# An encoder step with a dense pass over all experts: gelu values gated and split in their PSUM banks, a regrouped grid of gates, one one-hot factor made by ScalarE

## The chip, the cores and the metric

One core of one Trainium2 chip runs the whole program. The metric is the device time of one execution in microseconds, the lower the better; where several runs are given, it is their median. TensorE (PE) does matmuls and transposes, VectorE (DVE) elementwise work with two inputs, ScalarE (ACT) functions of one input, GpSimd (POOL) elementwise work and the issue of gathers, SyncE (SP) most of the transfers. Sums of products come out of PE in PSUM banks, everything else lives in SBUF.

## What is computed

The reference is one layer of a streaming encoder over 1024 prompt frames and 32 sample frames of 1024 channels: a token mixer (differential attention and a gated recurrence behind one projection), then PEER, a mixture of 16384 single-neuron experts with 8 heads of 16 chosen experts a frame. The change touches the second half:

```python
def blk(xs):
    q = (xs @ w_q).reshape(P_TBLOCK, P_HEADS, 2, P_DQ).astype(jnp.float32)
    s = jnp.einsum('thcd,hckd->thck', q, sub_keys.astype(jnp.float32))
    sv, si = lax.top_k(s, P_TOPK)
    comb = (sv[:, :, 0, :, None] + sv[:, :, 1, None, :]).reshape(P_TBLOCK, P_HEADS, P_TOPK * P_TOPK)
    cv, ci = lax.top_k(comb, P_TOPK)
    e = ...
    gate = jax.nn.softmax(cv, axis=-1)
    hid = jax.nn.gelu(jnp.einsum('thkd,td->thk', down[e], xs).astype(jnp.float32), approximate=False)
    return jnp.einsum('thk,thkd->td', (gate * hid).astype(xs.dtype), up[e])
```

So each frame adds, over its 128 chosen experts, gate times gelu of (expert's row of `down` dot the frame) times the expert's row of `up`.

## The kernel before, in words

The frames are nine tiles: 0 to 7 of 128 prompt frames each and "S" with the 32 sample frames. Tiles 0 to 4 (`DENSE`, 640 frames, `NV`) go through *all* experts by dense products; tiles 5, 6, S and 7 (`ROWS`) gather the rows of their chosen experts, 128 gathered rows a prompt tile and 32 for S (four frames' places side by side on the partitions), 416 in all.

**Streams.** Five generators are woven by the times that they yield: `gemm` (projection, output stages, and at its end the dense pass), `attn`, `routing` (top 16 of each head), `scatter` and `rows`. The order in which the instructions of an engine stand comes from this weave and from a scheduler over it; each engine then runs its own queue in order.

**Scatter.** For each dense tile the gates are laid on the grid of all experts. For four frames at a time (a step; 160 steps in all) one one-hot factor `ohA` (row of the expert) is made by DVE (L1126) in every second step and by ACT in the others (four times Abs, L1134, then Relu, L1135); the other factor `ohB` is made by DVE (L1126) and multiplied by the gates on POOL (L1139). PE multiplies them (L1090), ACT copies the bank to `stg` (L1091), and 16 frames at a time go to DRAM, `W_d`, laid out as [block of 8 columns, 128, frame, column].

**The dense pass** (`stage_v`) has 128 columns of 128 experts, in 32 groups of four (`JU`). For a column, `hidden` makes two halves of 320 frames: 24 matmuls into a bank (L261 to L263: a product of numbers in two parts each, high by high, low by high, high by low), and ACT puts gelu of the bank into `vg` in SBUF (L1174). `gated` multiplies `vg` by the gates `gw` on DVE, half by half (L1214; `gw` holds a frame's eight columns side by side, so one column is read at every eighth number), ACT copies the result to `vwh` (L254, 640 wide), DVE subtracts that for the low part `vwl` (L255, 640 wide). Then `down`'s weights of the group meet four columns at once: 8 pieces of the channels by 2 halves of frames are 16 products of 12 matmuls into banks `gv`, and DVE adds each to `acc` in SBUF (L1279). So a group is 384 matmuls of 320 columns, and its loop `for dq in range(4)` makes one column of the *next* group's hidden values and then four products of this group. `vwh` and `vwl` have six places (`WR`), `gv` has five banks, a sixth (`wsp`) serves the scatter and the tile S, two belong to the rows.

**Rows.** POOL issues a gather of 128 rows (L1044; four places `row`, `RB`), DVE makes the dot product with the frame (L1047), ACT gelu and gate (L1049, L1050), DVE adds the weighted row (L1031), always one row later than the dot. Columns 2 to 5 of the first hidden values lie in the place that `acc` takes later (`early`).

Of the kernel before, what the change touches and what calls it, by code (L numbers as in the profile page):

```python
# [7 lines left out]
F32 = mybir.dt.float32  # L8
# [4 lines left out]
OP = mybir.AluOpType  # L13
# [14 lines left out]
# tiles of frames that share a pass over w_in; tiles that share one over the other weights  # L28
AG = [[0, 1, 2, 3, 4], [5, 6, 7, "S"]]
CDG = [[0, 1, 2], [3, 4], [5, 6, 7, "S"]]  # L30
# tiles whose expert products run over all experts; the other ones gather the rows of theirs
# [3 lines left out]
# tiles whose scores wait in DRAM, and how many heads are routed at a time if not all  # L35
DEFER = [6, 7]
HG = {5: 2, 6: 4}
# places of weights in the rings, as they come and in two parts: output stages, then projections
RINGS = [(4, 4), (2, 3), (3, 4), (4, 4)]
SCS = [2, 2, 4, 3]  # L40
# places of the recurrence's tiles, by group
DEEP = [(2, 10), (1, 5)]
# frames on their way into the projections, by group
PRE = [2, 1]
# places of: gathered rows; expert weights, as they come and split; best halves; one-hots
RB, VR, VB, BB, OHB = 4, 3, 2, 4, 4
# engines that make the one-hot rows, in turn
AMS = "DA"
# of the splits of weights in the output stages, one in so many goes to the vector engine
CSH = 2  # L50
# banks of the large products: so many of so many in turn from the extra pool of that size
GX = (3, 6, 3)
# columns of experts whose hidden values wait in the place of the sums
GB, GE = 2, 6
# the time that a gathered row and a one-hot half step are taken to cost
GC, SC = 1.65, 1.0
# which streams keep behind the large products in which phase, and by how much less
# [10 lines left out]
def step_kernel(ctx, tc, x_prompt, x_sample, cache_kT, cache_v, state, norm1, w_in, lam_params,  # L68
# [27 lines left out]
    gb_bank, gv_bank = bank_of("gb"), bank_of("gv")  # L96
    TURN = [0]

    def gm_bank():
        """ the banks of the large products; more of them while the attention asks for none """  # L100
        TURN[0] += 1
        key = "gx" if "gx" in P and TURN[0] % GX[1] < GX[0] else "gm"
        return P[key].tile([128, 512], F32, name="gm", tag="gm")
# [7 lines left out]
    # ---------------------------------------------------------------- constants  # L111
# [7 lines left out]
    runs4 = consts.tile([128, 32], F32, name="runs4")  # L119
    V.tensor_add(runs4, ident[:, 0:32], ident[:, 32:64])  # L120
    V.tensor_add(runs4, runs4, ident[:, 64:96])
    V.tensor_add(runs4, runs4, ident[:, 96:128])
# [16 lines left out]
    def masks(ct):  # L139
        """ what the attention and the recurrence need of constants """  # L140
# [1312 lines left out]
```

## Time and profile before

| what | us |
|---|---|
| median of three runs | 3577.84 (3566.3 to 3578.75) |
| span of the profiled execution, its own time | 3583.5 |
| PE busy | 3257.4 (91%) |
| DVE busy | 3063.6 (85%) |
| POOL busy | 2074.9 (58%) |
| ACT busy | 1454.3 (41%) |

The span runs from the first to the last event of the profiled execution. For that execution no other time is given, so the span stands for it; it lies 5.7 us (0.16%) above the median. The mixer takes the first 1286 us, with scatter and rows beginning beside it; the dense pass takes from about 1585 us to the end. PE is busiest over the whole, but a share over the whole says little here: the stages have different limits, so they are read one by one below.

### The profile page before, as it was taken

The page shows a single profiled execution, that of the slowest core. Times are in us where ns is not written, and L with a number is a line of the kernel's source. Part 1 is how long each engine was busy: PE and PEld are TensorE (multiplying, and loading weights), DVE is VectorE, ACT ScalarE, POOL GpSimd, SP SyncE. Part 2 cuts the span into 40 slices and gives each one's busy share as a digit, 9 for nine tenths or more (in the row PEclk, how much of TensorE's full clock was granted, in tenths as well). Part 3 has the DMA queues.
Part 4 walks back from the last instruction along what each step waited for, and adds up shares of the span by engine and source line. Part 5 has one row for each costly group of instructions (what it writes and reads, how often), then busy time and mean ns, then how long its engine had stood idle before and what let it go on. Part 6 is the DMA issues. An engine that isn't in the chain of part 4 may idle for free.

```text
span 3583.5 us, 59911 instructions
## 1 busy us (share of the span) xinstructions
PE 3257.4 (91%) x21639; PEld 3128.0 (87%) x21639; DVE 3063.6 (85%) x6101; ACT 1454.3 (41%) x3508; POOL 2074.9 (58%) x1339
## 2 busy tenths in 40 slices
PE   7999899989998887868989988899999999999995
PEld 7989899867877886767889888899999999999994
DVE  3354468999787999999999999988989989989998
ACT  3544334445665544543333323333333333333332
POOL 2322125546444556666666577777767666776674
PEclk9999999999998998978999999999999999999997
DMA  4554364454465644478788777799888998998987
GB/s 164 166 158 149 107 215 158 152 151 152 148 217 183 206 130 150 152 249 298 258 289 296 275 271 290 266 341 351 316 315 335 337 343 296 346 338 333 336 325 265
DMA packets 357304, 880.58 MB, mean 246 GB/s; under 512 B 30960, under 2 KB 190192, under 8 KB 299664
## 3 DMA queue, kind: packets, MB, share of 16 engines
q1 hardware_dynamic: 297104, 440.52, 36.8%
q0 software_dynamic: 59904, 436.23, 33.0%
q8 instruction: 171, 2.80, 0.3%
q14 instruction: 125, 1.02, 0.1%
HBM read 784.47 MB, written 92.14 MB: 245 GB/s over the span
## 4 chain that ended last, share of the span: by engine, by line
PE 28%; DVE 19%; issue 2%; DMA 2%; POOL 2%; ACT 0%; POOLq 0%; ACTq 0%; DVEq 0%
PE gv L263 9%; PE gv L262 9%; PE gv L261 9%; DVE row L1047 5%; DVE xp L1031 5%; DVE vg L1214 2%; DVE acc L1279 2%; DMA ur<-in_p_up_dram 2%; DVE vwl L255 2%; POOL row L1044 1%; DVE oh L967 1%; POOL dl L255 1%; DVE ef L972 1%; POOL ul L255 0%; DVE si L902 0%
## 5 line engine op out<-in xcount | busy, mean ns | idle before, releaser
L1044 POOL DMA_INDIRECT row<-in_p_rows_dram,ei x384 | 559.8, 1458 | 340.2 <-DVE xp L1031 172.2
L255 POOL TENSOR_TENSOR wl<-wr,wh 128x1024 fp32r<-128x1024 f32 x160 | 397.3, 2494 | 532.2 <-ACT wh L254 483.0
L261 PE MATMUL gv<-vxh,dh 128*128 128x320 f32 x2048 | 646.5, 316 | 42.4 <-DVE acc L1279 23.6
L263 PE MATMUL gv<-vxh,dl 128*128 128x320 f32 x2048 | 644.8, 316 | 34.8 <-POOL dl L255 34.7
L261 PE MATMUL gv<-vwh,uh 128*128 128x320 f32 x2048 | 636.2, 311 | 14.1 <-ACT uh L254 8.3
L262 PE MATMUL gv<-vwl,uh 128*128 128x320 f32 x2048 | 636.8, 311 | 12.4 <-DVE vwl L255 12.3
L262 PE MATMUL gv<-vxl,dh 128*128 128x320 f32 x2048 | 642.3, 314 | 0.0
L263 PE MATMUL gv<-vwh,ul 128*128 128x320 f32 x2048 | 633.9, 310 | 1.1 <-POOL ul L255 1.0
L1047 DVE CUSTOM_DVE_ANT_0 row<-row,xg 128x1024 f32<-128x1024 f32 x416 | 627.0, 1507 | 3.1 <-DMA sc<-scs 2.3
L1031 DVE SCALAR_TENSOR_TENSOR xp<-row,hid,xp 128x1024 f32<-128x1024 f32 x412 | 527.8, 1281 | 78.2 <-ACT hid L1050 78.0
L1049 ACT ACTIVATE hid<-hid 128x1 f32<-128x1 f32 x416 | 84.0, 202 | 936.1 <-DVE hid L1047 926.3
L255 POOL TENSOR_TENSOR ul<-ur,uh 128x512 fp32r<-128x512 f32 x256 | 359.7, 1407 | 135.2 <-ACT uh L254 125.6
L261 PEld LDWEIGHTS gv<-vxh,dh 128*128 128x128 f32 x2048 | 393.5, 192 | 50.1 <-DVE acc L1279 27.3
L263 PEld LDWEIGHTS gv<-vxh,dl 128*128 128x128 f32 x2048 | 392.7, 192 | 43.1 <-POOL dl L255 42.0
L255 POOL TENSOR_TENSOR dl<-dr,dh 128x512 fp32r<-128x512 f32 x256 | 365.1, 1433 | 82.0 <-ACT dh L254 73.9
L261 PEld LDWEIGHTS gv<-vwh,uh 128*128 128x128 f32 x2048 | 386.7, 189 | 17.1 <-ACT uh L254 9.3
L262 PEld LDWEIGHTS gv<-vwl,uh 128*128 128x128 f32 x2048 | 386.9, 189 | 16.5 <-DVE vwl L255 16.5
L262 PEld LDWEIGHTS gv<-vxl,dh 128*128 128x128 f32 x2048 | 393.9, 192 | 0.0
L263 PEld LDWEIGHTS gv<-vwh,ul 128*128 128x128 f32 x2048 | 386.3, 189 | 2.7 <-POOL ul L255 2.5
L1139 POOL TENSOR_TENSOR ohB<-ohB,tr 128x512 f32<-128x512 f32 x160 | 195.0, 1224 | 264.3 <-DVE ohB L1126 201.5
L1214 DVE TENSOR_TENSOR vg<-vg,gw 128x320 f32<-128x320 f32 x248 | 253.4, 1022 | 27.7 <-ACT vg L1174 17.5
L261 PE MATMUL gm<-xh,wh 128*128 128x320 f32 (+1 forms) x768 | 254.0, 331 | 0.0
(328 smaller groups left out, 7490.5 us busy)
## 6 DMA issues: line engine op xcount, KB each, us to landing
dr<-in_p_downT_dram SPq DMA_DIRECT2D x256, 256.0 KB
ur<-in_p_up_dram SPq DMA_DIRECT2D x256, 256.0 KB
wr<-in_w_in_dram SPq DMA_DIRECT2D x88, 512.0 KB
W_d<-stg SPq DMA_DIRECT2D x40, 1024.0 KB
gw<-W_d SPq DMA_DIRECT2D x32, 1280.0 KB
wr<-in_p_wq_dram SPq DMA_DIRECT2D x48, 512.0 KB
wr<-in_w_out_dram SPq DMA_DIRECT2D x24, 512.0 KB
wr<-in_w_a_dram SPq DMA_DIRECT2D x12, 512.0 KB
```

The lines of the kernel that those rows point to most:

```text
L255: (lo_engine or G).tensor_tensor(out=l, in0=src, in1=h.bitcast(F32), op=OP.subtract)
L261: PE.matmul(out, lh, rh, start=(i == 0), stop=False)
L262: PE.matmul(out, lh, rl, start=False, stop=False)
L263: PE.matmul(out, ll, rh, start=False, stop=(i == n - 1))
L967: V.tensor_tensor(out=oh[:T], in0=cf[:T, h].unsqueeze(2).to_broadcast([T, 16, NCAND]), in1=iota_c[:T].unsqueeze(1).to_broadcast([T, 16, NC ...
L1031: V.scalar_tensor_tensor(out=acc, in0=row[:, D:], scalar=hid[:, k:k + 1], in1=acc if k else first, op0=OP.mult, op1=OP.add)
L1044: G.indirect_dma_start(out=row, out_offset=None, in_=p_rows, in_offset=bass.IndirectOffsetOnAxis(ap=ei[:, k:k + 1], axis=0))
L1047: V.tensor_tensor_reduce(out=row[:, 0:D], in0=row[:, 0:D], in1=xt, scale=1.0, scalar=0.0, op0=OP.mult, op1=OP.add, accum_out=h)
L1049: A.activation(h, h, AF.Gelu)
L1139: G.tensor_tensor(out=bm, in0=bm, op=OP.mult, in1=tr[:, 2, xs].unsqueeze(2).to_broadcast([128, 4, 128]))
L1214: V.tensor_mul(gh, gh, G_[h][:, :, j])
L1279: V.tensor_add(acc[:, db, cs], acc[:, db, cs], ps[:, :CHUNK])
```

## The change

- **Values in banks.** From column 6 on, gelu writes back into its PSUM bank; the gate is multiplied on the bank (bank in, bank out); high and low parts are split from it in two pieces of 320 instead of one of 640. There is no `vg` any more, and a bank is free only when both parts have been read. Every sixth bank of the dense pass is now `wsp`'s, so there are six. Columns 0 to 5 use `early`.
- **Gates by runs of 16.** `W_d` and `gw` are laid out as [.., run, column, 16 frames]; a column is read in runs of 16 numbers, and `stg` is written accordingly.
- **One-hot factor.** `ohA` is made by ACT in all 160 steps: 80 DVE instructions go, and 320 Abs and 80 Relu come to ACT.
- **Rows.** Five places for gathered rows, and the add follows two rows behind the dot. For S, three transfers and three adds take the place of a product with a constant. The routing of the `ROWS` tiles starts only after that of all dense tiles is done with.

```diff
-RB, VR, VB, BB, OHB = 4, 3, 2, 4, 4
+RB, VR, VB, BB, OHB = 5, 3, 2, 4, 4
...
+    def gv_bank():
+        TURN[0] += 1
+        pool, tag = (wsp, "ws") if PHASE[0] and TURN[0] % 6 == 0 else (P["gv"], "gv")
+        return pool.tile([128, 512], F32, name="gv", tag=tag)
...
-                if late:
-                    add(*late)
-                late = (k, row)
+                if len(late) > 1:
+                    add(*late.pop(0))
...
-                for c in range(2):
-                    ps = ws_bank()
-                    PE.matmul(ps[:T], runs4, full[:, c * 512:(c + 1) * 512], start=True, stop=True)
-                    V.tensor_add(ht[:T, c * 512:(c + 1) * 512], ht[:T, c * 512:(c + 1) * 512], ps[:T])
+                pw = wide("runs")
+                V.tensor_add(ht[:T], ht[:T], acc[:T])
+                for g, part in enumerate((pw[:, 0:D], pw[:, D:], sq)):
+                    SP.dma_start(out=part[:T], in_=full[(g + 1) * T:(g + 2) * T])
+                    V.tensor_add(ht[:T], ht[:T], part[:T])
...
-    W_d = dram([128 // JB, 128, NV, JB], "W_d")
+    W_d = dram([128 // JB, 128, NV // SB, JB, SB], "W_d")
...
+                   or (t in ROWS and not all(x in DONE for x in DENSE))
...
-                    if AMS[(s0 + q) // 4 % len(AMS)] == "A":
-                        for u in range(4):
-                            c = s0 + q + u
-                            A.activation(am[:, u], iota_r, AF.Abs, bias=tr[:, 3, c:c + 1])
-                        A.activation(am, am, AF.Relu, bias=1.0, scale=-1.0)
-                    else:
-                        equal(am, 0)
-                    equal(bm, 1)
+                    for u in range(4):
+                        c = s0 + q + u
+                        A.activation(am[:, u], iota_r, AF.Abs, bias=tr[:, 3, c:c + 1])
+                    A.activation(am, am, AF.Relu, bias=1.0, scale=-1.0)
...
-        if GB <= e < GE:
-            g = VX["early"][:, e - GB]
-        else:
-            g = wk.tile([128, NV], F32, name="vg", tag="vg", bufs=GB)
+        VX[e] = []
         for cs in CS:
             ps = gv_bank()
...
-            A.activation(g[:, cs], ps[:, :CHUNK], AF.Gelu)
-        VX[e] = g
+            g = VX["early"][:, e, cs] if e < GE else ps[:, :CHUNK]
+            A.activation(g, ps[:, :CHUNK], AF.Gelu)
+            VX[e].append(g)
...
-                g = VX[e]
-                for h in range(2):
-                    gh = g[:, h * (n // 2):(h + 1) * (n // 2)]
-                    V.tensor_mul(gh, gh, G_[h][:, :, j])
...
-                split(wh, wl, g, V)
+                for cs, g, gates in zip(CS, VX[e], G_.values()):
+                    gt = g.rearrange("p (m s) -> p m s", s=SB)
+                    V.tensor_tensor(out=gt, in0=gt, in1=gates[:, :, j], op=OP.mult)
+                    split(wh[:, cs], wl[:, cs], g, V)
```

How the program's order moves is shown at the end of one group of the dense pass. First DVE's queue before, over the last four products of one group (`acc` sums, `gv` banks, `row` and `xp` the gathered rows, `vwl` low parts of the next group's hidden values; the numbers tell one buffer from another):

```order
L1279 TENSOR_TENSOR acc_17249<-acc_17249,gv_33348 128x320
L1031 SCALAR_TENSOR_TENSOR xp_29497<-row_30330,hid_29496,xp_29497 128x1024
L1279 TENSOR_TENSOR acc_17249<-acc_17249,gv_33362 128x320
L1047 ISA row_30336,hid_29496<-row_30336,xg_29494 128x1024
L1047 ISA hid_29496 128x1
L1279 TENSOR_TENSOR acc_17249<-acc_17249,gv_33382 128x320
L255 TENSOR_TENSOR vwl_33176<-vg_33120,vwh_33175 128x640
L1279 TENSOR_TENSOR acc_17249<-acc_17249,gv_33396 128x320
L255 TENSOR_TENSOR vwl_33339<-vg_33283,vwh_33338 128x640
L1031 SCALAR_TENSOR_TENSOR xp_29497<-row_30336,hid_29496,xp_29497 128x1024
```

The low parts of two columns of the next group are taken from `vg` in SBUF, in two pieces. The changed kernel's queue at the end of a group:

```order
L1274 TENSOR_TENSOR acc_17575<-acc_17575,gv_32455 128x320
L1274 TENSOR_TENSOR acc_17575<-acc_17575,gv_32503 128x320
L1047 ISA row_31377,hid_29894<-row_31377,xg_29892 128x1024
L1047 ISA hid_29894 128x1
L1274 TENSOR_TENSOR acc_17575<-acc_17575,gv_32469 128x320
L1031 SCALAR_TENSOR_TENSOR xp_29895<-row_31377,hid_29894,xp_29895 128x1024
L255 TENSOR_TENSOR vwl_32283<-gv_32230,vwh_32282 128x320
L255 TENSOR_TENSOR vwl_32283<-gv_32256,vwh_32282 128x320
L255 TENSOR_TENSOR vwl_32442<-gv_32389,vwh_32441 128x320
L1274 TENSOR_TENSOR acc_17575<-acc_17575,gv_32489 128x320
L255 TENSOR_TENSOR vwl_32442<-gv_32415,vwh_32441 128x320
```

They are now taken from banks (`gv_32230`, `gv_32256`, `gv_32389`, `gv_32415`) in four pieces, all behind the sum of the next to last product (`gv_32469`), so four banks are held until here.

PE's queue before, at the turn from the next to last product of a group (`gv_33382`) to the last one (`gv_33396`), with the semaphores that each row waits for:

```order
L261 MATMUL gv_33382<-vwh_32683,uh_33378 128x320
L262 MATMUL gv_33382<-vwl_32684,uh_33378 128x320
L263 MATMUL gv_33382<-vwh_32683,ul_33379 128x320
L261 MATMUL gv_33396<-vwh_32194,uh_33378 128x320 [waits Activation_49]
L262 MATMUL gv_33396<-vwl_32195,uh_33378 128x320
L263 MATMUL gv_33396<-vwh_32194,ul_33379 128x320
```

The last product's bank waits only for ACT, which had emptied it as a hidden half long before. The same turn after the change, from `gv_32469` to `gv_32489`:

```order
L261 MATMUL gv_32469<-vwh_31786,uh_32451 128x320
L262 MATMUL gv_32469<-vwl_31787,uh_32451 128x320
L263 MATMUL gv_32469<-vwh_31786,ul_32452 128x320
L261 MATMUL gv_32489<-vwh_31295,uh_32485 128x320 [waits DVE_49]
L262 MATMUL gv_32489<-vwl_31296,uh_32485 128x320
L263 MATMUL gv_32489<-vwh_31295,ul_32486 128x320
```

Its first matmul now waits for DVE; what it waits for is the sum of the bank of the product directly ahead, since no other bank is free. And the turn behind the last product, where the next group's hidden half begins:

```order
L261 MATMUL gv_32489<-vwh_31786,uh_32485 128x320
L262 MATMUL gv_32489<-vwl_31787,uh_32485 128x320
L263 MATMUL gv_32489<-vwh_31786,ul_32486 128x320
L261 MATMUL gv_32553<-vxh_16916,dh_32543 128x320 [waits DVE_49]
L262 MATMUL gv_32553<-vxl_16917,dh_32543 128x320
L263 MATMUL gv_32553<-vxh_16916,dl_32544 128x320 [waits Pool_49]
```

That first matmul also waits for DVE, for the low part `vwl_32283` of the earlier column. In the changed program this pattern stands in each of the 31 groups that make hidden values for a next one.

Counted in the two programs: ahead of the first sum of the dense pass stand 31 dots of gathered rows before and 46 after; from there to the end of the eighth group 97 and 111. The last gathered row stands at the program's end before, and in group 28 (of 0 to 31) after.

## Rows read from the trace of the kernel before

**Rows 1.** Windows by stage: stretch, length, busy (count) of PE PEld DVE ACT POOL, PEclk, DMA share, GB/s.
```profile
744.00:1300.00 556.00, 494.42 (x3343) 438.94 (x3341) 488.88 (x1156) 306.33 (x736) 283.06 (x167) 0.94 0.56 173
1300.00:1706.00 406.00, 319.18 (x1967) 303.09 (x1966) 382.36 (x954) 193.63 (x458) 257.79 (x161) 0.88 0.60 204
1706.00:2243.00 537.00, 479.50 (x3076) 466.06 (x3075) 536.08 (x1003) 169.12 (x435) 360.97 (x244) 0.97 0.78 280
2243.00:2370.00 127.00, 116.65 (x772) 114.53 (x771) 120.91 (x158) 41.69 (x106) 100.83 (x65) 0.97 0.81 295
2370.00:3397.00 1027.00, 1018.73 (x6917) 1013.79 (x6916) 932.92 (x1205) 368.46 (x956) 719.66 (x512) 1.00 0.90 330
3397.00:3584.00 187.00, 142.84 (x955) 139.85 (x953) 164.62 (x235) 58.60 (x162) 115.55 (x82) 0.89 0.80 299
```

**Rows 2.** Windows, an undisturbed stretch of three and a half groups, columns as in rows 1.
```profile
2400.00:2600.00 200.00, 200.00 (x1366) 200.00 (x1365) 181.60 (x237) 74.89 (x193) 147.33 (x105) 1.00 0.91 334
```

**Rows 3.** Groups of DVE by form in 1706 to 2243: busy, mean ns, idle before.
```profile
L1047 DVE CUSTOM_DVE_ANT_0 row<-row,xg 128x1024 f32<-128x1024 f32 x99 | 155.4, 1570 | 0.0
...
L1214 DVE TENSOR_TENSOR vg<-vg,gw 128x320 f32<-128x320 f32 x64 | 73.1, 1144 | 0.0
...
L255 DVE TENSOR_TENSOR vwl<-vg,vwh 128x640 fp32r<-128x640 f32 x33 | 49.0, 1486 | 0.4 <-ACT vwh L254 0.4
```

**Rows 4.** Waits of PE in 1706 to 2243: us in total, times, longest.
```profile
PE gv L261 <- DVE acc L1279: 28.0, 17, 5.3
```

**Rows 5.** Timeline at 3545, the last matmul of the last product.
```profile
3545.54 0.31 PE L263 MATMUL gv<-vwh,ul 128*128 128x320 f32 x1
```

**Rows 6.** Groups of DVE by form in 3546 to 3584.
```profile
L1047 DVE CUSTOM_DVE_ANT_0 row<-row,xg 128x1024 f32<-128x1024 f32 x7 | 13.8, 1965 | 0.4 <-DMA row<-in_p_rows_dram,ei 0.4
L1031 DVE SCALAR_TENSOR_TENSOR xp<-row,hid,xp 128x1024 f32<-128x1024 f32 x7 | 9.0, 1280 | 0.0
```

**Rows 7.** Groups of DVE by form in 744 to 1300.
```profile
L1126 DVE TENSOR_TENSOR ohA<-iota_r,tr 128x512 f32<-128x512 f32 x48 | 38.2, 796 | 6.7 <-PE ws L1090 6.5
```

**Rows 8.** Groups of ACT by form in 744 to 1300.
```profile
L254 ACT ACTIVATE wh<-wr 128x1024 fp32r<-128x1024 f32 x66 | 69.3, 1056 | 37.7 <-DMA wr<-in_p_wq_dram 13.1 <-PE gm L262 8.3 <-DMA wr<-in_w_out_dram 6.2
L1134 ACT ACTIVATE ohA<-iota_r,tr 128x128 f32<-128x128 f32 x188 | 59.7, 394 | 0.0
...
L1135 ACT ACTIVATE ohA<-ohA 128x512 f32<-128x512 f32 x47 | 29.4, 625 | 0.2
```

**Rows 9.** Groups of DVE by form in 1300 to 1706.
```profile
L1047 DVE CUSTOM_DVE_ANT_0 row<-row,xg 128x1024 f32<-128x1024 f32 x29 | 49.8, 1716 | 2.3 <-DMA sc<-scs 2.3
L1031 DVE SCALAR_TENSOR_TENSOR xp<-row,hid,xp 128x1024 f32<-128x1024 f32 x27 | 34.5, 1278 | 10.4 <-ACT hid L1050 10.4
L1126 DVE TENSOR_TENSOR ohA<-iota_r,tr 128x512 f32<-128x512 f32 x32 | 32.1, 1004 | 1.4 <-PE ws L1090 1.4
```

**Rows 10.** One line's and one tile's instructions, whole program: min/median/max ns.
```profile
L1279 DVE TENSOR_TENSOR acc<-acc,gv x496: 423/476/514, 1716.4 to 3549.5; 128x320 f32<-128x320 f32 x166
...
L1214 DVE TENSOR_TENSOR vg<-vg,gw x248: 702/805/2767, 1586.0 to 3496.6; 128x320 f32<-128x320 f32 x124
```

**Rows 11.** Timeline at 3149, end of one product: start, us, instruction, idle before.
```profile
3148.83 0.31 PE L263 MATMUL gv<-vwh,ul 128*128 128x320 f32 x1
...
3149.18 0.49 DVE L1279 TENSOR_TENSOR acc<-acc,gv 128x320 f32<-128x320 f32 x1 [0.18 <-PE gv L263]
```

**Rows 12.** Timeline at 1801, a bank that PE waits for.
```profile
1801.44 0.47 DVE L1279 TENSOR_TENSOR acc<-acc,gv 128x320 f32<-128x320 f32 x1
...
1801.96 0.42 PE L261 MATMUL gv<-vxh,dh 128*128 128x320 f32 x1 [1.35 <-DVE acc L1279]
```

**Rows 13.** Timeline at 2161, the longest of such waits.
```profile
2161.34 0.64 PE L261 MATMUL gv<-vxh,dh 128*128 128x320 f32 x1 [5.34 <-DVE acc L1279]
```

**Rows 14.** Windows right behind these two waits, columns as in rows 1.
```profile
1801.90:1806.00 4.10, 4.04 (x27) 4.04 (x28) 4.10 (x10) 0.20 (x1) 3.62 (x3) 1.00 0.99 388
2161.30:2163.30 2.00, 1.96 (x7) 1.96 (x8) 2.00 (x17) 0.47 (x2) 1.71 (x2) 0.50 0.55 86
```

## What I expect, and why

> **What bounds the kernel now.** I read first the windows by stage [rows 1], since shares over the whole mix stages with different limits. The reader is to look in each row for the engine that fills its stretch. From 744 to 1300 us PE (494 of 556) and DVE (489) are close to each other. From 1300 to 1706 DVE is the fullest (382 of 406). From 1706 to 2243 DVE has 536 of 537 us: DVE is the limit. From 2370 to 3397 it is PE, 1019 of 1027. How many groups of the dense pass a stretch has follows from its matmuls, 384 each: 3076 are 8 groups, 772 are 2, 6917 are 18.
>
> What a group costs where only PE counts is read from a stretch without any idle time of PE: 1366 matmuls in 200 us, 146.4 ns each [rows 2], so 384 take 56.2 us. The eight groups in which DVE is the limit take 67.1 us each, the next two 63.5, the eighteen 57.1. Their excess over 56.2 is 87, 15 and 15 us: that is what relief of DVE can bring there.
>
> Next come DVE's groups by form in the stretch that it limits [rows 3]: a gathered row's dot takes 1.57 us, a gate (64 of them) 1.144, a low part of 640 columns (33) 1.486. The waits of PE there name DVE's sum into `acc` [rows 4]: a bank is not yet emptied. At the end, the last product's matmul ends at 3545.85 [rows 5], 37.7 us before the span ends, and seven gathered rows, 13.8 + 9.0 us of DVE, lie in that tail [rows 6].
>
> The sum is made against the profiled execution's 3583.5 us, 5.7 above the median of the runs; I subtract 5.7 at the end.
>
> **The change, stretch by stretch.**
>
> *744 to 1300.* Of the steps of the scatter, 48 lose their `ohA` on DVE, 0.796 us each [rows 7]: −38. ACT makes them by four Abs and a Relu, 4 × 0.394 + 0.625 = 2.2 us [rows 8]: +106, from 306 to 412 of 556, still 74%. PE's own 494 us is next in line, so DVE's 38 us can't all come off: bounds are 0 and −38, and since PE and DVE were nearly equal I take −10.
>
> *1300 to 1706.* DVE loses 32 `ohA` (−32) and most of the 10.4 us in which an add waits for its row's hidden value from ACT [rows 9], because the add now comes two rows behind (−8); a few gates get cheaper (−3). But it gets 15 more rows ahead of the first sum (46 against 31, by the program's order): 15 × (1.716 + 1.278) = +45 [rows 9]. That gives +2, and for ACT, which makes 70 us more here (194 to 264 of 406) in a queue that gelu and the splits share, I add 3: +5, between −15 and +20.
>
> *1706 to 2243, eight groups, limited by DVE.* The trace of before shows no multiplication on a bank. The nearest row is the sum into `acc`: one input from a bank, one from SBUF, 320 columns, 423/476/514 ns (shortest, middle, longest) over all 496 [rows 10]. The gate of before, both inputs in SBUF and one of them at every eighth number, has 702/805/2767. A gate on the bank has the sum's shape except that it writes to the bank, and it reads runs of 16; so I take 0.476, with the old middle value 0.805 as the upper bound. A low part of 320 columns also has one input from a bank and one from SBUF: 0.476, bounded by half of today's, 0.743. Gates: 64 × (1.144 − 0.476) = −42.8. Low parts: 33 × 1.486 = 49.0 go, 66 × 0.476 = 31.4 come, −17.6. Rows move into these groups (111 against 97 dots by the order): 14 × 1.57 + 15 × 1.28 = +41. With +7 for the wait described next, as far as it isn't hidden by DVE's own queue, this is −12; bounds: −30 (no wait, part of the rows hidden) and +27 (upper bounds of both prices).
>
> On the prices the Trainium skill bears, in "SBUF — State Buffer", section "Who interferes with whom": an instruction of VectorE with at most one input in SBUF doesn't contend with GpSimd, one with two inputs there does. The trace agrees: the sums never took over 514 ns, the gates up to 2767 [rows 10]. By the rule 0.476 holds with POOL busy as well; without it the sum would be 39 us higher, worked out below as a rival.
>
> *The wait that comes.* The order of the changed program shows it: `vwh` and `vwl` have six places and the group under way uses four, so two of the next group's columns are split at once and the other two, four banks of six, wait until the group's last product has used its places. So its last four products share two banks. The last one starts in the bank of the product directly ahead, and PE waits for DVE's sum of that. Before, those banks had been emptied a long time earlier. The price: a matmul ends 0.31 us after its start, while the next could start after 0.146, so 0.164 us are lost; DVE's sum starts 0.04 later (3148.83 + 0.31 = 3149.14, then 3149.18) and takes 0.49 [rows 11]; PE starts 0.05 after it (1801.44 + 0.47 = 1801.91, then 1801.96) [rows 12]. Together 0.74 us, if DVE is free. A dot in front of the sum can add up to 1.57; I take 0.9 on average, between 0.74 and 2.3. The next group's first hidden half waits for low parts on DVE at the same turn; the queue has these ready just as the last product ends, so I put this at nothing, with 0.3 as the other bound.
>
> *2243 to 2370, two groups.* DVE's 121 us become about 106 (a group has 8 gates and 4 low parts: 8 × 0.668 + 4 × 1.486 − 8 × 0.476 = 7.5 us less), so PE is the limit: 2 × (56.2 + 0.9) = 114 against 127, −13.
>
> *2370 to 3397, eighteen groups, limited by PE.* Relief of DVE brings nearly nothing here, the wait costs 18 × 0.9 = +16; of the 15 us lost today I let 4 go: +12, between 0 and +40.
>
> *3397 to the end.* The rows end in group 28, so their 22.8 us leave the tail; but the last sums, transposes and norms stand there too, and partly beside them: −16, and −2 for waits in the last groups. −18, between −10 and −22.
>
> S's three transfers with adds instead of a product, and the other order of routing, cost nothing: the tile's end lies beside the dense pass, and what the routing moves is in the rows counted above. The transfers of `W_d` and `gw` keep their bytes, and the groups ahead of their use cover them as before; without that cover each of the 15 later loads would cost a wait of DVE, which no row here prices.
>
> Sum: −10 + 5 − 12 − 13 + 12 − 18 = −36; 3583.5 − 36 − 5.7 = **3542 us**.
>
> **Rivals.**
> *No wait, full relief.* DVE's 38 us come off whole, +2 in the second stretch, −19 without the wait in the eight groups, then −15, −15, −18: −103, 3475 us. For it: DVE is as full as PE at 744 and the wait is short. Against it: the order makes PE wait in all 31 groups. Chance 0.10.
>
> *ACT holds back the products.* 66 splits of weights on ACT feed PE in the first stretch [rows 8]; each may now stand behind the five instructions of a step, 2.2 us, on average half of that: 66 × 1.1 = 73, half of it covered by the ring of weights: +36 there in place of −10, so 3542 + 46 = 3588 at worst, and with some of it hidden 3580. For it: ACT already had 306 us and half of the steps. Against: 74% is not full. Chance 0.18.
>
> *The wait drags the clock down (slower).* Behind a wait of 5.34 us [rows 13] the granted clock was 0.50, 1.2 GHz, and 2 us there had 7 matmuls instead of 14; behind one of 1.35 us it stayed at 1.00, 2.4 GHz [rows 14]. If DVE is late by another us at each turn and the clock falls for some 4 us, a group loses 1 + 2 us more: 20 × 3 = +60, 3602 us. Without any wait the sum is −54, so it is zero at 2.7 us a group and +18 at 3.6. Chance 0.16. This side is taken by a rule of the Trainium skill, "PSUM — Partial Sum Buffer", "Summary: rules for kernel authors": evacuate promptly. The change keeps values in banks through gelu, gate and split, so by that rule it comes out slower, as in this case; the trace so far has 28 us of waits for banks in eight groups [rows 4], though a sum empties its bank at once.
>
> *Gates and low parts on banks stay dear.* 64 × 0.33 + 66 × 0.27 = +39: 3581 us. Against it: the 514 ns. Chance 0.06.
>
> **How the numbers follow.** The forecast has 0.50; its own range, from the bounds above, is 3515 to 3575. The measurement of this kernel can tell about 0.5%, 18 us, from no change. Faster than 3560: 0.43 of the forecast, 0.10 of full relief, 0.03 of the others, 0.56. Slower than 3596: 0.11 of the clock, 0.03 of ACT, 0.02 of the rest, 0.16. Between: 0.28. The range 3500 to 3600 leaves out full relief (0.10) and half of the clock's case (0.08).
>
> **What would show it.** Right: gates and low parts near 0.48 us; eight groups near 65 us; a wait of PE for DVE of 0.7 to 1 us ahead of the last product in every group, and groups of 57 us after 2370; no rows in the tail. Wrong: gates over 0.6 us; waits over 2 us with a clock below 1.00 in the late groups; a scatter that ends later than 1604 because ACT is full; or groups of 56.2 us, if no wait appears.

## The result, and the profile after

The changed kernel takes 3605.0 us (median of 4 runs, 3604.3 to 3605.9) against 3578.3: a ratio of 1.007 with an interval of 1.0047 to 1.0094, slower by 26.7 us where 36 us less were forecast. (The 3578.3 is the median of the kernel before over four runs.) The profiled execution's span is 3602.5 us, 19.0 more than before; the rest of the 26.7 is there because the profiled execution of the kernel before was slower than its median. Windows by stage of the changed kernel, cut where its own groups begin (group 1, 9, 11 and 29 of the dense pass), columns as in [rows 1]:

```profile
744.00:1300.00 556.00, 494.61 (x3297) 438.82 (x3298) 453.32 (x1104) 385.62 (x973) 275.85 (x168) 0.92 0.55 172
1300.00:1737.70 437.70, 317.95 (x2005) 304.39 (x2004) 398.00 (x993) 251.30 (x657) 269.00 (x178) 0.86 0.66 231
1737.70:2280.60 542.90, 484.50 (x3074) 475.58 (x3073) 532.92 (x1091) 186.81 (x495) 382.29 (x267) 0.93 0.83 306
2280.60:2395.90 115.30, 113.89 (x771) 112.62 (x770) 100.84 (x148) 43.13 (x120) 80.47 (x60) 1.00 0.94 354
2395.90:3443.80 1047.90, 1025.73 (x6914) 1016.82 (x6914) 858.39 (x1314) 389.73 (x1044) 714.70 (x516) 1.00 0.89 329
3443.80:3602.50 158.70, 138.77 (x954) 138.00 (x952) 51.85 (x106) 39.93 (x85) 58.16 (x46) 0.95 0.26 87
```

The cuts of [rows 1] from 1706 on are the same groups of the kernel before, so the lengths can be compared row by row: group 1 begins 31.4 us later (1737.7 against 1706.3), the eight groups take 542.9 against 537, the next two 115.3 against 127, the eighteen 1047.9 against 1027, the end 158.7 against 187 (to 3602.5 against 3584). Nearly the whole loss stands before group 1 and in the eighteen groups.

The prices on which the forecast rested came out as taken. DVE's groups by form in the eight groups (columns as in [rows 3]), then two rows of the lists by tile (as in [rows 10]):

```profile
L1047 DVE CUSTOM_DVE_ANT_0 row<-row,xg 128x1024 f32<-128x1024 f32 x112 | 177.3, 1583 | 1.9 <-DMA row<-in_p_rows_dram,ei 1.9
L1031 DVE SCALAR_TENSOR_TENSOR xp<-row,hid,xp 128x1024 f32<-128x1024 f32 x114 | 145.3, 1275 | 1.1 <-ACT hid L1050 1.1
...
L1211 DVE TENSOR_TENSOR gv<-gv,gw 128x320 f32<-128x320 f32 x65 | 31.4, 483 | 0.5 <-ACT gv L1169 0.5
L255 DVE TENSOR_TENSOR vwl<-gv,vwh 128x320 fp32r<-128x320 f32 x65 | 29.8, 476 | 1.0 <-ACT vwh L254 1.0
...
L967 DVE TENSOR_TENSOR oh<-cf,iota_c 32x800 f32<-32x800 f32 x8 | 11.3, 1417 | 0.0
...
L972 DVE TENSOR_REDUCE ef<-oh 32x16 f32<-32x800 f32 x8 | 7.7, 968 | 1.5 <-POOL oh L970 1.5
```

```profile
L1211 DVE TENSOR_TENSOR gv<-gv,gw x244: 461/495/500, 1705.1 to 3543.8; 128x320 f32<-128x320 f32 x122
...
L255 DVE TENSOR_TENSOR vwl<-gv,vwh x244: 459/482/493, 1730.0 to 3552.0; 128x320 fp32r<-128x320 f32 x122
```

The gate is 0.483 us (0.476 taken), the low part 0.476, and none of 244 is over 0.500: the 42 and 19 us did come off DVE in the eight groups. But 112 dots and 114 adds stand there now, 40 us more than before, and the last two rows of the first list, of S's routing, are 14 us more than before. The kernel before had 99 dots there [rows 3], 2.9 and 1.9 us of the two rows of S's routing, and these adds:

```profile
L1031 DVE SCALAR_TENSOR_TENSOR xp<-row,hid,xp 128x1024 f32<-128x1024 f32 x100 | 127.5, 1275 | 0.2 <-ACT hid L1050 0.2
```

So DVE is about as full as it was, 533 us.

The wait that the order foretold is there. Waits of PE in the eighteen groups, then one turn to a group's last product, start, us, instruction, idle before:

```profile
PE gv L261 <- DVE acc L1274: 20.7, 20, 3.5
PE gv L261 <- DVE vwl L255: 1.1, 5, 0.4
```

```profile
3028.63 0.31 PE L263 MATMUL gv<-vwh,ul 128*128 128x320 f32 x1
...
3028.98 0.49 DVE L1274 TENSOR_TENSOR acc<-acc,gv 128x320 f32<-128x320 f32 x1
...
3029.52 0.42 PE L261 MATMUL gv<-vwh,uh 128*128 128x320 f32 x1 [0.58 <-DVE acc L1274]
```

A matmul ends at 3028.94, the sum runs to 3029.47, PE starts 0.05 later: 0.58 us of idle time, with the 0.164 of the drain the 0.74 of the forecast. Twenty such waits in eighteen groups sum to 20.7 us.

### The profile page after: what moved, and what is told of

It is laid out like the page before. It is cut to its first block, busy times and chain, and to the rows that moved or that the text cites. A ratio compares the mean times of both kernels' runs of the same rounds, so it can differ in the third digit from the quotient of the medians.

```text
span 3602.5 us, 60487 instructions
## 1 busy us (share of the span) xinstructions
PE 3259.8 (90%) x21635; PEld 3135.7 (87%) x21635; DVE 2834.6 (79%) x6148; ACT 1614.2 (45%) x4034; POOL 2018.5 (56%) x1339
## 4 chain that ended last, share of the span: by engine, by line
PE 57%; DVE 28%; DMA 4%; issue 4%; ACT 3%; POOL 2%; SPq 0%; DVEq 0%; ACTq 0%; POOLq 0%
PE gv L261 12%; PE gv L262 11%; PE gv L263 11%; PE gm L261 6%; PE gm L263 6%; PE gm L262 6%; DVE row L1047 5%; DVE xp L1031 5%; DVE acc L1274 2%; DVE oh L967 2%; PE ws L1093 1%; DVE ohB L1132 1%; DVE ef L972 1%; PE gb L468 1%; DMA row<-in_p_rows_dram,ei 1%
## 5 line engine op out<-in xcount | busy, mean ns | idle before, releaser
L261 PE MATMUL gv<-vwh,uh 128*128 128x320 f32 x2048 | 648.3, 317 | 96.7 <-DVE acc L1274 63.9
L1044 POOL DMA_INDIRECT row<-in_p_rows_dram,ei x384 | 514.3, 1339 | 259.1 <-DVE xp L1031 141.7
L1047 DVE CUSTOM_DVE_ANT_0 row<-row,xg 128x1024 f32<-128x1024 f32 x416 | 599.4, 1441 | 3.1 <-DMA row<-in_p_rows_dram,ei 2.1
L255 POOL TENSOR_TENSOR ul<-ur,uh 128x512 fp32r<-128x512 f32 x256 | 368.0, 1438 | 181.6 <-ACT uh L254 162.3
L1274 DVE TENSOR_TENSOR acc<-acc,gv 128x320 f32<-128x320 f32 x496 | 235.4, 479 | 93.5 <-PE gv L263 90.2
L254 ACT ACTIVATE uh<-ur 128x512 fp32r<-128x512 f32 x256 | 161.2, 630 | 301.3 <-PE gv L262 209.3
```

What stands on the lines that cost most here:

```text
L254: A.activation(h, src, AF.Copy)
L255: (lo_engine or G).tensor_tensor(out=l, in0=src, in1=h.bitcast(F32), op=OP.subtract)
L261: PE.matmul(out, lh, rh, start=(i == 0), stop=False)
L1044: G.indirect_dma_start(out=row, out_offset=None, in_=p_rows, in_offset=bass.IndirectOffsetOnAxis(ap=ei[:, k:k + 1], axis=0))
L1047: V.tensor_tensor_reduce(out=row[:, 0:D], in0=row[:, 0:D], in1=xt, scale=1.0, scalar=0.0, op0=OP.mult, op1=OP.add, accum_out=h)
L1274: V.tensor_add(acc[:, db, cs], acc[:, db, cs], ps[:, :CHUNK])
```

## The experiments

Start of group 1, lengths of stretches and dots from group 29 on are read from each trace at the first product of a group (in e3, where the first two matmuls of group 1 stand ahead of a hidden half, behind that half, so that all rows count the same work):

| run | us, median | ratio (interval) | group 1 at | groups 1–8 | 11–28 | 29 to end | dots before group 1 / in 1–8 / from 29 on |
|---|---|---|---|---|---|---|---|
| before | 3578.3 | 1 | 1706 | 537 | 1027 | 186 | 30 / 98 / 39 |
| after | 3605.0 | 1.007 (1.0047–1.0094) | 1738 | 543 | 1048 | 159 | 45 / 112 / 0 |
| e1 | 3582.0 | 1.0012 (1.0003–1.0022) | 1723 | 547 | 1029 | 160 | 42 / 96 / 27 |
| e2 | 3572.3 | 0.9987 (0.9976–0.9999) | 1706 | 544 | 1048 | 159 | 33 / 109 / 12 |
| e3 | 3581.7 | 1.0016 (1.0001–1.0031) | 1735 | 530 | 1040 | 159 | 39 / 108 / 8 |
| e4 | 3540.2 | 0.9886 (0.9867–0.9906) | 1715 | 516 | 1013 | 172 | 37 / 96 / 33 |
| e5 | 3588.9 | 1.0032 (1.0018–1.0045) | 1704 | 565 | 1046 | 159 | 28 / 113 / 11 |
| e6 | 3551.6 | 0.9926 (0.9907–0.9946) | 1680 | 526 | 1014 | 204 | 26 / 99 / 45 |
| e7 | 3557.9 | 0.9947 (0.9928–0.9967) | 1690 | 519 | 1013 | 199 | 26 / 100 / 43 |
| e8 | 3547.5 | 0.9910 (0.9891–0.9929) | 1697 | 514 | 1017 | 188 | 30 / 98 / 38 |
| e9 | 3526.8 | 0.9849 (0.9833–0.9866) | 1724 | 499 | 1017 | 171 | 38 / 97 / 32 |
| e10 | 3543.5 | 0.9902 (0.9885–0.9919) | 1716 | 514 | 1014 | 171 | 38 / 95 / 33 |
| e11 | 3541.5 | 0.9894 (0.9875–0.9913) | 1728 | 498 | 1018 | 176 | 40 / 95 / 31 |
| e12 | 3524.6 | 0.9847 (0.9821–0.9873) | 1686 | 499 | 1015 | 205 | 27 / 99 / 44 |

Two theories stood for the late start. Theory 1: gathered rows that the order puts ahead of the dense pass delay it. Theory 2: ScalarE, now with all one-hot factors, holds the scatter back. For the eighteen groups the theory was the held banks.

**e1, the one-hot edit alone, in the kernel before.**

```diff
-AMS = "DA"
+AMS = "A"
```

> The kernel before with one edit: all one-hot factors by ScalarE. By the program's order this alone puts 44 dots of gathered rows (31 before) ahead of the first sum. Theory 1 (the order: rows are put ahead of the scatter's last steps and of the first gates): the second group of the dense pass starts 15 to 30 us later than 1706, the scatter ends about 30 us later than 1591, and the whole is 0 to 20 us slower than before. Theory 2 (ScalarE itself is full and holds the scatter back): the same direction, but the loss is spread over 744 to 1530 as well, 20 to 40 us. Rival: ScalarE's steps cost nothing, then the time is within 5 us of before or faster.

It costs 0.1%. The list of DVE's sums in this run gives the first and the last sum's start:

```profile
L1279 DVE TENSOR_TENSOR acc<-acc,gv x496: 456/477/522, 1735.9 to 3563.5; 128x320 f32<-128x320 f32 x166
```

The first sum is at 1735.9, against 1716.4 in [rows 10]: the edit alone delays the start (17 us by the table, 42 dots ahead instead of 30). It comes back at the end: 27 dots from group 29 on instead of 39, and 26 us less there.

**e2, the one-hot edit undone in the changed kernel.**

```diff
-                    for u in range(4):
-                        ...
+                    if (s0 + q) // 4 % 2:
+                        for u in range(4):
+                            ...
+                    else:
+                        V.tensor_tensor(out=am, ..., in1=tr[:, 0, xs]..., op=OP.is_equal)
```

> The changed kernel with one edit: one-hot factors by VectorE and ScalarE in turn again. 33 dots stand ahead of the first sum instead of 46. If the one-hot edit is what delays the dense pass, its second group starts near 1706 instead of 1738 and the whole comes to 3570 to 3585, 20 to 35 us below the changed kernel. If the delay is another part's, the time stays within 10 us of 3605.

As expected: group 1 begins at 1706 again, and the whole is 33 us shorter. So the same edit costs 33 us here and nearly nothing in e1. The end tells why: here it takes 159 us either way, with 12 dots in it or none, so rows that leave it earn nothing.

**e3 and e4, four places for rows; then banks freed by the gate.** e3 has `RB` 4 instead of 5. e4 adds:

```diff
+                vg = wk.tile([128, n], F32, name="vg", tag="vg", bufs=2)
...
-                    V.tensor_tensor(out=gt, in0=gt, in1=gates[:, :, j], op=OP.mult)
-                    split(wh[:, cs], wl[:, cs], g, V)
+                    vt = vg[:, cs].rearrange("p (m s) -> p m s", s=SB)
+                    V.tensor_tensor(out=vt, in0=gt, in1=gates[:, :, j], op=OP.mult)
+                    split(wh[:, cs], wl[:, cs], vg[:, cs], V)
```

> The changed kernel with four places for gathered rows instead of five (the base for the next run). 39 dots ahead of the first sum instead of 46. By theory 1 the start of the dense pass is some 10 us earlier and the whole 3590 to 3605; if the fifth place matters for itself, the rows wait and the whole is over 3605.

> The run above with one more edit: the gate still reads the bank, but writes to SBUF, so a bank is free after its gate; the low parts are split from SBUF. If the wait at each group's end is for held banks, groups from the twelfth on take 56.3 us instead of 57.1 to 58.3, no wait of TensorE for VectorE's sum is left there, and the whole is 20 to 35 us below the run above. If the waits have another cause, groups stay above 57 us and the time is the same or, by dearer low parts (0.74 us against 0.48 where VectorE is the limit), up to 15 us longer.

Without the fifth place the whole is 23 us shorter, more than expected, and not where it was expected: 39 dots stand ahead of group 1, not 45, but it begins only 3 us earlier; the eight groups take 13 us less and the eighteen 8. e4 is 41 us below e3, 26 of them in the eighteen groups. Its group 1 begins 20 us earlier with nearly the same number of dots ahead (37), so the number alone doesn't set the start; what else does isn't shown. PE's waits in the eighteen groups of e3:

```profile
PE gv L261 <- DVE acc L1274: 14.1, 18, 1.6
```

and the window of the same groups in e4 (columns as in [rows 1]):

```profile
2353.20:3366.50 1013.30, 1013.30 (x6914) 1013.30 (x6913) 883.47 (x1281) 385.44 (x1030) 681.08 (x513) 1.00 0.90 335
```

18 waits for the sums in 18 groups before, none after: PE is busy in every one of the 1013.3 us. The waits were for held banks.

**e5, the changed kernel with rows kept back.**

```diff
-AHEADS = dict(rows=60.0)
+AHEADS = dict(rows=-20.0)
```

> The changed kernel with one number changed: gathered rows may not run ahead of the dense products by 60 us but stay 20 us behind. 28 dots stand ahead of the first sum instead of 46; all one-hot factors are still ScalarE's. Theory 1 (rows ahead of the first gates delay the dense pass): its second group starts at 1700 to 1712 instead of 1738 and the whole comes to 3570 to 3590. Theory 2 (ScalarE holds the scatter back): the second group still starts after 1725 and the whole stays within 10 us of 3605.

Theory 1 holds for the start: the first product of group 1 comes at 1704 with ScalarE making every one-hot factor. The scatter's last one-hot on DVE still begins late, as the list by tile shows:

```profile
L1132 DVE TENSOR_TENSOR ohB<-iota_r,tr x160: 659/684/2924, 742.6 to 1624.3; 128x512 f32<-128x512 f32 x160
```

1624 against 1630 in the changed kernel. But that one-hot is not the end of the scatter: behind it come PE's product, ACT's copy to `stg`, the transfer to `W_d` and the load of the gates. The last copies and the first gates that use the second load, in the changed kernel and then in e5:

```profile
1652.12 0.60 ACT L1094 ACTIVATE stg<-ws 128x512 f32<-128x512 f32 x1 [1.02 <-PE ws L1093]
...
1678.15 3.58 DVE L1211 TENSOR_TENSOR early<-early,gw 128x320 f32<-128x320 f32 x6
```

```profile
1635.26 0.60 ACT L1094 ACTIVATE stg<-ws 128x512 f32<-128x512 f32 x1 [1.11 <-PE ws L1093]
...
1646.86 3.58 DVE L1211 TENSOR_TENSOR early<-early,gw 128x320 f32<-128x320 f32 x6 [2.80 <-DMA gw<-W_d]
```

So of the 33 us, 17 are won at the scatter's end and 14 more between it and these gates: in the changed kernel DVE makes dots and adds of rows up to the gates, in e5 it waits for the gates' load. Rows ahead put off both.

The time is at the upper edge of what was expected: the eight groups take 565 us, 22 more, with DVE busy for 548 of them, 15 more, the dots being dearer there (1.70 us against 1.58). Of 33 us won at the start, 16 are left in the median.

**e6 and e7, the same number of rows ahead with and without the one-hot edit.** Both are e4; e6 has one-hot factors by both engines as in e2, e7 rows kept back as in e5.

> The run with the gate from bank to SBUF and four places for rows, with one-hot factors by both engines in turn. 26 dots ahead of the first sum instead of 39. By theory 1 the start gains some 10 to 20 us and the eight groups limited by VectorE some more, as there is more of them left for later: 3520 to 3540. If ScalarE is what matters, the gain is the same; if neither, 3540 and above.

> As the run above, but with one-hot factors by ScalarE alone and rows kept 20 us behind: 27 dots ahead of the first sum. Theory 1: the same time as the run above within 8 us, since it has the same rows ahead. Theory 2: 15 us or more slower than it.

With 26 dots ahead in both, group 1 begins at 1680 and 1690, and the whole differs by 6 us (their profiled spans by 2, the other way). That leaves some 10 us for ScalarE's steps. It is no clean price: the rows stand at other places in the two runs, 8 dots ahead of the scatter's last copy in e6 and 15 in e7, and that copy comes at 1592.5 and 1622.0. Both are slower than e4, where e6 was expected to be faster: with rows kept back 43 to 45 dots are left from group 29 on, and the end takes 199 to 204 us. A row put early costs time, and one left for the end does too beyond the 27 or so that the end hides (it takes 160 us with 27 dots in e1, 159 with none in the changed kernel); in the eighteen groups DVE has room for it.

**e8, the grid of gates in runs of 16, alone in the kernel before.**

```diff
-    W_d = dram([128 // JB, 128, NV, JB], "W_d")
+    W_d = dram([128 // JB, 128, NV // SB, JB, SB], "W_d")
...
-                    gh = g[:, h * (n // 2):(h + 1) * (n // 2)]
-                    V.tensor_mul(gh, gh, G_[h][:, :, j])
+                    gh = g[:, h * (n // 2):(h + 1) * (n // 2)].rearrange("p (m s) -> p m s", s=SB)
+                    V.tensor_tensor(out=gh, in0=gh, in1=G_[h][:, :, j], op=OP.mult)
```

> The kernel before with one part of the change: the grid of gates in runs of 16 frames; gates are still multiplied in SBUF. If the old gate's price is its stride of eight numbers, a gate falls from 0.805 to about 0.57 (middle value) and the eight groups limited by VectorE lose 10 to 25 us, the whole 3555 to 3570. If its price is two inputs in SBUF beside GpSimd, its mean there stays above 0.9 and the whole within 8 us of before.

31 us less from this part alone, more than expected; in the profiled executions 23 go in the eight groups, 9 ahead of them and 10 in the eighteen. The gate in the list by tile and, in the eight groups, by form:

```profile
L1215 DVE TENSOR_TENSOR vg<-vg,gw x248: 459/485/2464, 1578.8 to 3457.7; 128x320 f32<-128x320 f32 x124
```

```profile
L1215 DVE TENSOR_TENSOR vg<-vg,gw 128x320 f32<-128x320 f32 x64 | 52.0, 814 | 0.0
```

The middle value falls from 0.805 to 0.485, as on a bank. The mean in the eight groups falls from 1.144 by as much, but only to 0.814 with both inputs in SBUF, longest 2.464, while on a bank it is 0.483, longest 0.500. There the stride and the second input in SBUF cost about a third of a microsecond each. The second is not paid beside the gathers themselves: of the 248 gates in e8, the 165 beside which POOL did nothing, or only issued a gather, took at most 0.500 us; the 83 beside other work of POOL, mostly its subtractions for the low parts of weights, took 1.14 on average. The longest one:

```profile
1878.54 2.55 POOL L255 TENSOR_TENSOR dl<-dr,dh 128x512 fp32r<-128x512 f32 x2
...
1878.98 2.46 DVE L1215 TENSOR_TENSOR vg<-vg,gw 128x320 f32<-128x320 f32 x1
```

**e9, seven places of parts instead of six, on e3.**

```diff
-    JU, WR = 4, 6
+    JU, WR = 4, 7
```

> The changed kernel with four places for gathered rows and seven places of high and low parts instead of six (gates and low parts still on banks): three of the next group's columns can be split at once, so two banks are held to the group's end, not four. If the waits come from the number of held banks, groups from the twelfth on take 56.3 us, waits of TensorE for the sums nearly go, and the whole is 3515 to 3545. If two held banks are enough to cause them, groups stay at 57 to 58 us and the whole is above 3565.

One number takes 55 us off e3. Windows of the eight and of the eighteen groups, and waits in the latter:

```profile
1723.80:2223.10 499.30, 464.48 (x3074) 460.29 (x3073) 479.67 (x1038) 172.83 (x461) 343.69 (x244) 0.97 0.82 299
2343.30:3360.30 1017.00, 1014.04 (x6914) 1013.31 (x6913) 861.01 (x1277) 383.52 (x1027) 688.55 (x512) 1.00 0.90 332
```

```profile
PE gv L261 <- DVE acc L1274: 1.8, 2, 1.0
```

With two banks held instead of four the waits are gone (2 instead of 18), 23 us in the eighteen groups. The eight groups take 30 us less than in e3, and group 1 begins 11 us earlier. The same groups in e3:

```profile
1734.60:2264.40 529.80, 477.09 (x3073) 468.83 (x3072) 513.06 (x1077) 185.32 (x486) 382.14 (x261) 0.95 0.82 304
```

The 30 us go with DVE's work more than with the wait: 480 us there against 513, with 97 dots instead of 108. The order that came out of seven places leaves these rows for later; 32 stand from group 29 on, and the end takes 12 us more.

**e10 and e11.** e10 is e4 with the low part in one piece of 640 columns; e11 is e9 with eight places, and two instead of three for the products' raw weights, to make room.

> The run with the gate from bank to SBUF, with the low part in one piece of 640 columns instead of two of 320. Two pieces took 2 x 0.871 us in the eight limited groups, one piece of before 1.486: 32 x 0.26 = 8 us less there; 3528 to 3540. No difference if what hides the low parts is as long: within 4 us of 3540.

> The changed kernel with four places for gathered rows, eight places of high and low parts and two places instead of three for the raw weights of the products: no bank is held beyond its own split, and gates and low parts stay on banks (0.48 us each). If held banks are the whole loss of the dense pass, its groups from the twelfth on take 56.3 us, the eight limited groups 490 to 510 us together, and the whole is 3500 to 3530. If values in banks cost something else as well, 3540 or more. If the third place for raw weights was needed, TensorE waits for the split of those weights.

e10 is no better than e4 (its 8 us aren't there). e11 missed its 3500 to 3530. It has the short eight groups, 498 us, and eighteen groups without waits for the sums, but its group 1 begins 5 us later than e9's and its end is 5 us longer; it is 15 us slower in the median and 10 in the profiled executions. By the expectation's own words, 3540 or more would mean that values in banks cost something else as well; whether it is that, or the missing place for raw weights, wasn't tried apart.

**e12, the one-hot edit undone once more, on e9.**

> The run with seven places of parts, with one-hot factors by both engines in turn again; 27 dots ahead of the first sum instead of 39. In the changed kernel this edit gained 33 us, since its last rows were through before the end anyway. Here 32 rows stand behind the twenty-ninth group. Theory (rows moved forward are paid where VectorE is the limit and only come back where they leave the end): the second group starts 25 to 35 us earlier, the end takes 20 to 35 us longer, and the whole is 0 to 15 us slower than with ScalarE alone, 3525 to 3542. Rival (one-hot factors on ScalarE cost for themselves): 3490 to 3505.

```profile
L1279 DVE TENSOR_TENSOR acc<-acc,gv x496: 450/476/490, 1692.2 to 3475.8; 128x320 f32<-128x320 f32 x166
```

The first sum comes at 1692.2 (1730 in e9): group 1 starts 38 us earlier, the end takes 34 us longer with 44 dots in it instead of 32, and the whole is the same within 2 us. What was worth 33 us in e2 is worth nothing where the end still has rows to lose. e9 and e12 are 1.5% below the kernel before, and so below the changed one too.

## Why the prediction was wrong

**The stretches to group 1 (−10 and +5 forecast, +31 measured): the step that failed.** I took what comes off DVE as time won (10 of the 38 us, then 32), and the 15 more rows as time of DVE alone (+45), and came out near nothing. Neither held. From 744 us to group 1 DVE's busy time did fall, by 20 us, but its idle time rose by 52. In the first stretch alone 36 us came off, and 36 came back as idle time, 16 of them in the scatter's own steps, which wait for PE's product of the scatter: 6.7 us at `ohA` [rows 7] and 5.7 at `ohB` before, 28.5 at `ohB` after. From 744 to 1300, before and after:

```profile
L1126 DVE TENSOR_TENSOR ohB<-iota_r,tr 128x512 f32<-128x512 f32 x96 | 94.5, 987 | 5.7 <-PE ws L1090 5.7
```

```profile
L1132 DVE TENSOR_TENSOR ohB<-iota_r,tr 128x512 f32<-128x512 f32 x94 | 88.8, 947 | 28.5 <-PE ws L1093 26.7 <-ACT tr L1117 1.5
```

The scatter was no further at 1300 for it (94 of these steps against 96). In the second stretch DVE's busy time rose by 16 us and its idle time by 16 (24 of 406 us in [rows 1], 40 of 437.7). Here I read the code of the rows wrongly, and the text on the change says it too: the new lines also add one row behind the dot, not two. So the −8 was never there; DVE's groups by form from 1300 to 1737.7 in the changed kernel show that wait grown, not gone:

```profile
L1047 DVE CUSTOM_DVE_ANT_0 row<-row,xg 128x1024 f32<-128x1024 f32 x45 | 62.6, 1394 | 0.2 <-DMA row<-in_p_rows_dram,ei 0.2
L1031 DVE SCALAR_TENSOR_TENSOR xp<-row,hid,xp 128x1024 f32<-128x1024 f32 x42 | 53.8, 1282 | 14.6 <-ACT hid L1050 13.7 <-DVE xp L1031 0.5
```

The rows themselves took 32 us more of DVE there, less than the +45. What I left out is where they stand: 25 dots instead of 11 lie ahead of the scatter's last copy, which comes at 1652.1 instead of 1603.8, and more lie ahead of the gates behind it. e2 takes the one-hot edit back and e5 holds the rows back; both bring the start back to 1706 and 1704. That the rows ahead carry most of the loss is shown by these two; how it is shared between DVE's time, the gathers and ScalarE's own steps isn't, since e6 and e7 differ in the rows' places too, and e3 and e4 begin 20 us apart with 39 and 37 dots.

My second rival named ScalarE and the splits of weights. The products that these feed were not held back: the last of them begin at 1508 us after and at 1517 before, with ScalarE at 386 of 556 us in the first stretch. The scatter did end later than 1604, which I had named as that rival's sign; but with ScalarE not full and more rows ahead, the sign alone doesn't speak for it.

**The eight groups (−12 forecast, +6 measured).** Gates (−42) and low parts (−19) came as worked out; rows came as +40, as worked out. What I left out stands on DVE too: the routing of S, +14. DVE's busy time so fell by 3 us instead of 19, and its idle time rose from 1 to 10, about the 7 that I had allowed for the wait. Waits of PE for the sums there grew from the 28 us of [rows 4] to 51.1:

```profile
PE gv L261 <- DVE acc L1274: 51.1, 20, 6.6
```

With DVE busy for 533 of 543 us these are a sign of its fullness more than a loss of their own. What could be saved there are the rows that the order puts in, as e9's 480 us of DVE show. S's routing is the term that I had put at nothing, as counted with the rows.

**The next two groups (−13)** came as −11.

**The eighteen groups (+12 forecast, +21 measured).** The mechanism and its smallest price held: 0.74 us. The average of 0.9 was too small. The groups take mostly 57.1 to 58.3 us, 1 to 2 us more than 56.2, because in about half of them a dot or an add stands ahead of the sum, as here, and the wait is 1.1 to 1.4 us:

```profile
2500.60 0.31 PE L263 MATMUL gv<-vwh,ul 128*128 128x320 f32 x1
...
2500.62 1.22 DVE L1047 CUSTOM_DVE_ANT_0 row<-row,xg 128x1024 f32<-128x1024 f32 x1
...
2501.78 0.48 DVE L1274 TENSOR_TENSOR acc<-acc,gv 128x320 f32<-128x320 f32 x1
...
2502.31 0.41 PE L261 MATMUL gv<-vwh,uh 128*128 128x320 f32 x1 [1.40 <-DVE acc L1274]
```

And one wait of 3.49 us took the clock along, which cost a group of 64.6:

```profile
2907.82 0.63 PE L261 MATMUL gv<-vwh,uh 128*128 128x320 f32 x1 [3.49 <-DVE acc L1274]
```

```profile
2907.80:2911.00 3.20, 3.18 (x12) 3.17 (x12) 2.70 (x4) 0.00 (x0) 1.37 (x1) 0.50 1.04 414
```

Granted clock 0.50, 1.2 GHz: 12 matmuls in 3.2 us instead of 22. The rival of the falling clock happened in one of eighteen groups, and its 20 × 3 us did not come.

**The end (−18 forecast, −28 measured)**: more rows had left it than the seven that I priced: 39 dots stand from group 29 on before, none after.

On the whole, the likeliest case's parts behind group 1 sum to −31 as forecast and to −12 as measured, and the start made it a loss. The rule on inputs in SBUF from the Trainium skill ("SBUF — State Buffer", "Who interferes with whom") is borne out by e8 against the changed kernel, 0.814 against 0.483, and by the 83 gates of e8 beside POOL's other work. Its advice to evacuate a bank promptly ("PSUM — Partial Sum Buffer", "Summary: rules for kernel authors"), which I weighed as the slower rival, points the right way: e4 and e9, which free banks earlier, have next to no such waits in the eighteen groups (none and two). What the held banks cost in those groups is 23 us by e9 and 26 by e4, both against e3, whose granted clock there was 1.00: it is the waits, not the clock.

Left open is why the order puts eleven more rows into the eight groups with six places of parts (108 dots in e3) than with seven (97 in e9). The same code with another `WR` gives another order; what in the scheduling makes it so wasn't tried. The routing's condition and S's sums by transfers weren't tried apart.

## What to carry to other kernels

Filler work that must be done anyway costs its time where its engine is the limit, and more where it stands ahead of something that others wait for, and nothing where another engine is the limit: ask of an edit not what it takes off an engine but where the order will put the filler then, and whether the place that it leaves was still paying. A value that stays in a bank until something else is released turns a short lack of places into a wait at every turn; count the held banks at the fullest moment, and add a place where it is cheapest (here a seventh place of parts took 55 us off, and giving up the fifth place of rows 23). And try the parts alone: the layout of the gates, the part that looked smallest, was worth 31 us by itself.

## What the runs showed of the hardware

A gate with both inputs in SBUF, read in runs of 16, took 0.485 us in the middle (e8). Beside nothing on GpSimd, or only the issue of a gather, it took at most 0.500; beside GpSimd's elementwise work it took 1.14 on average and up to 2.46. With one input in a bank it was never over 0.500 in the changed kernel. Reading one input at every eighth number instead of in runs of 16 took the middle value to 0.805. Of TensorE's waits for sums in the eighteen groups of the changed kernel, those between 0.58 and 1.4 us were followed by a granted clock of 1.00, but for one of 0.58 us directly behind the longest, where the clock had already fallen; the longest, 3.49 us, was followed by 0.50.
